# Attention by half chunks in two turns between the output products of a hybrid decoder layer

## The chip, the cores and the metric

The kernel runs on one core of one Trainium2 chip. Its engines are TensorE (PE in the profile, its weight loads PEld), VectorE (DVE), ScalarE (ACT), GpSimd (POOL) and SyncE (SP), which issues most DMAs. The metric is the device time of one execution in microseconds (us), as the median of the runs shown.

## The reference, cut to what matters

One layer: a normalised input is projected once, three head groups work on the result, and one output projection follows. Two of the groups are attentions:

```
q, k, v      8 query heads, 2 key/value heads (4 queries each), head_dim 64, 4096 tokens
window:      banded blocks of 128 queries against 256 keys (the block before and its own),
             mask 0 <= i + 128 - j < 128, softmax with one sink logit per head, * silu(gate)
memory:      4 heads of 64 against 256 memory tokens, softmax, * silu(gate)
y = concat(conv 256, window 512, memory 256) @ w_out;   out = x + rmsnorm(y) * norm_post
```

A second, small batch (8 x 8 tokens against cached keys) goes through the same layer, and the new keys, values and states are returned.

## The kernel before, in words

**Stages.** Three phases compute the input projection (line L368, tiles `c`), the last of them together with the memory keys and the attention of the first 256 tokens. Up to about 930 us that is all; the rest is attention and output projection, and this is the part that changes.

**Precision.** Most products are made from a high and a low part of each operand in the float32r type. For the window scores a head's 128 contraction rows hold the query's high part in one half of 64 rows and its low part in the other, against the key's high part (part 0 of `kst`) in both halves, and then against the key's low part (part 1): two products of 128 rows x 256 keys for each head and block of 128 queries. The products with the values (`wo`) are plain float32.

**Chunks and halves.** The 4096 tokens are 16 chunks of 256 (`Chunk`, c from 0), each with two blocks of 128 queries (i = 0, 1). I call block i of chunk c the half h = 2c + i. Halves 0 and 1 are done in the input projection, so that 30 are left.

**Steps of one half.**
- Window scores `ws` (L1246): for each key/value head (kvh) 4 heads x 2 parts, 16 products into four one-bank PSUM tiles. ACT copies the own block's columns (L1248), DVE puts the previous block's columns over them under a mask (L1249), then maximum (L1251), exponentials (L1259, sink L1256), sum, reciprocal and factor (L1264), all in tile `sm`.
- Transposes `wt` (L1269) of `sm`; ACT copies them out (L1271), and two selections on POOL make the two triangles (L1276, L1279).
- Memory scores `xs` (L1182) for 2 heads, maximum (L1183), exponentials (L1186), factor on POOL (L1191), transposes `xt` (L1197), and copies out, half by DVE and half by ACT (L1201).
- Products with the values (`wo`, L1088 for memory, L1218 and L1224 for the window) in column tiles and 64 x 64 tiles of TensorE, two or four at once, and two gates on DVE (L1170, L1227).

**Order.** `pairs` cuts a chunk into eight units (window and memory in turn, one for each kvh or memory head). `Pipe.start` begins one unit, puts the transposes of the unit begun two starts earlier on the queue, and after each pair its products. The output projection of a block of 128 tokens, `Block.run`, is 2 parts of 24 products of 512 columns (`y`, L1492); it calls `start` ahead of k = 2 and k = 6 of each part (0, 2, 4, 6 in the first two blocks), so at four places in a block. A scheduler at build time fixes the order of the instructions on every engine of this stage.

**Memory.** PSUM's eight banks: tags `s`, `t` and `z` (the `y` sums) with two banks each, and `pv`, one tile of two banks. Keys and queries of chunk c + 1 are loaded from DRAM by POOL's queue while chunk c is worked on, the gates (`mix`) by SP's. The small batch's attention (`sample_mem`, `sample_window`) is spread over blocks 26 to 30.

Of the kernel before, what the change touches and what calls it, by code (L numbers as in the profile page):

```python
# [52 lines left out]
def hybrid_layer(ctx: ExitStack, tc: tile.TileContext, a: dict):  # L53
# [951 lines left out]
    def open_attention():  # L1005
# [7 lines left out]
        ps = {tag: ctx.enter_context(tc.tile_pool(name=f"ps{tag}", bufs=1 if tag == "pv" else 2, space=bass.MemoryType.PSUM))  # L1013
              for tag in ("s", "t", "z", "pv")}
# [19 lines left out]
    def psum(tag, name):  # L1034
        if ps is None:
            return third["ps"].tile([P, 512], F32, tag="m", name=name)
        if tag == "pv":

            return ps[tag].tile([P, 2, 512], F32, tag=tag, name=name)[:, 0]
        return ps[tag].tile([P, 512], F32, tag=tag, name=name)  # L1040
# [6 lines left out]

    class Pipe:

        def __init__(self):
            self.waiting, self.due, self.t = [], {}, 0

        def add(self, pair):

            left, right, both = pair
            self.waiting += [(left, None), (right, both)]

        def start(self):
            values, transposes, factors = self.due.pop(self.t, ([], [], []))
            at = lambda n: self.due.setdefault(self.t + n, ([], [], []))
            if self.waiting:
                unit, both = self.waiting.pop(0)
                next(unit)
                at(1)[2].append(unit)
                at(2)[1].append(unit)
                if both is not None:
                    at(3)[0].append(both)  # L1070
            for fn in values:
                fn()
            for unit in (*transposes, *factors):
                next(unit, None)
            self.t += 1

        def drain(self):
            while self.waiting or self.due:
                self.start()
# [10 lines left out]
    class Chunk:  # L1090


        def __init__(self, c):
            self.c = c
            self.t0 = NS + CT * c
            self.ts = slice(self.t0, self.t0 + CT)
# [18 lines left out]
        def load_queries(self):  # L1115

            self.q = self.pool("q").tile([P, 12, CT], F32R, tag="q", name=f"q{self.c}")
            for part in range(2):
                for hh in range(2):
                    half = hh if part == 0 else 1 - hh  # L1120
                    G.dma_start(self.q[half * 64 : half * 64 + 64, hh::2, :],  # L1121
                                  qd[part, 1:7, hh * 64 : hh * 64 + 64, self.ts].rearrange("j p n -> p j n"))
# [34 lines left out]
        def cross_pair(self, j, band_values):  # L1157
# [4 lines left out]
            def both():  # L1162
                banks = ps["pv"].tile([P, 2, 512], F32, tag="pv", name=f"wo{c}_{j}") if c else None
# [10 lines left out]
        def cross_unit(self, h, pts):  # L1174
            c, nb = self.c, CT // P
            q = self.q[:, h]
            p = work([P, nb, 256], "p", f"xp{c}_{h}")
            mx, nm, den, rd = (tiny.tile([P, 4], F32, tag=n, name=f"x{n}{c}_{h}") for n in ("mx", "nm", "den", "rd"))
            s = psum("s", f"xs{c}_{h}").rearrange("p (b k) -> p b k", b=nb)
            for i in range(nb):  # L1180
                for part in range(2):
                    TE.matmul(s[:, i, :], q[:, i * P : i * P + P], third["mk"][:, part, h, :], start=part == 0, stop=part == 1)  # L1182
# [4 lines left out]
            V.reciprocal(rd[:, :nb], den[:, :nb])  # L1187
            yield 1
            for i in range(nb):

                G.tensor_scalar(p[:, i, :], p[:, i, :], rd[:, i : i + 1], 0.5, op0=ALU.mult, op1=ALU.mult)  # L1191
            yield 1
            pt = work([P, 2, CT], "xpt", f"xpt{c}_{h}")
            for kt in range(2):
                t = psum("t", f"xt{c}_{h}_{kt}")
# [253 lines left out]
    class Block:  # L1449
# [26 lines left out]
        def run(self, last, start, split, starts):  # L1476
# [6 lines left out]
            for p, (c0, c1) in enumerate(parts):  # L1483
                if p == 1:
                    split()
# [197 lines left out]
```

## Time and profile before

| what | value |
|---|---|
| median of 3 runs | 1538.47 us (1533.01 to 1540.08) |
| the profiled execution: its own time, span of the core | 1536.4 us, 1534.7 us |
| granted TensorE clock | 1.00 |
| busy: PE, PEld, DVE, ACT, POOL | 99%, 91%, 75%, 52%, 25% |
| DMA | 306.28 MB, mean 200 GB/s |

The profiled execution is one run; its own time is 2.1 us under the median. Busy time of PE is taken from modelled ends of pipelined matmuls, so that a matmul's duration (0.28 us for 256 columns) is longer than the distance from its start to the next one's. The text below reads distances between starts.

### The profile page before, as it was taken

The numbers are of one execution on the slowest core, as the hardware profiler recorded it, in microseconds if no ns is written. First come the engines' busy times: TensorE is split into PE (matmuls) and PEld (weight loads), VectorE is DVE, ScalarE is ACT, GpSimd is POOL, SyncE is SP. The second block draws the span as 40 slices with busy tenths as digits, with TensorE's granted clock in tenths as the row PEclk, the third lists the DMA queues.
The fourth block names the chain that finished last, engine by engine and source line by source line (L and its number), as shares of the span: only waits on it lengthen the run. The fifth ranks groups of instructions, "written<-read, shape, count | busy, mean of one in ns | idle before, by whom it ended". The sixth has DMA issues, their size and how long they took to land.

```text
span 1534.7 us, 30168 instructions
## 1 busy us (share of the span) xinstructions
PE 1521.5 (99%) x11341; PEld 1399.5 (91%) x11341; DVE 1145.5 (75%) x2055; ACT 805.7 (52%) x2039; POOL 376.1 (25%) x603
## 2 busy tenths in 40 slices
PE   9999999999999999999999999999999999999998
PEld 9999999999999999999999998788888888888877
DVE  6788887899988777897777678766666666666743
ACT  6675665475322222354454447655666556565632
POOL 0223332211300000000101203544444444444310
PEclk9999999999999999999999999999999999999999
DMA  9989999878855333677877789977777777777333
GB/s 265 194 222 225 283 284 266 272 242 298 193 181 180 126 126 126 220 230 280 227 273 230 229 293 254 231 161 153 156 148 148 151 162 149 158 160 150 130 110 96
DMA packets 177942, 306.28 MB, mean 200 GB/s; under 512 B 33925, under 2 KB 107653, under 8 KB 177765
## 3 DMA queue, kind: packets, MB, share of 16 engines
q1 hardware_dynamic: 130901, 227.38, 48.2%
q0 software_dynamic: 46176, 75.92, 25.5%
q8 instruction: 90, 1.47, 0.4%
q10 hardware_dynamic: 720, 1.05, 0.2%
q14 instruction: 55, 0.45, 0.1%
HBM read 197.23 MB, written 108.05 MB: 199 GB/s over the span
## 4 chain that ended last, share of the span: by engine, by line
PE 86%; DMA 7%; DVE 4%; issue 1%; ACT 1%; POOL 1%; SPq 0%; ACTq 0%; DVEq 0%; POOLq 0%
PE c L368 47%; PE y L1492 23%; PE ws L1246 4%; DMA nat<-in_x_p 3%; DMA md<-th 2%; PE wo L1088 2%; PE wt L1269 2%; PE xs L1182 2%; PE xt L1197 2%; PE wo L1218 2%; PE wo L1224 1%; PE mem_acc L789 1%; DMA qd<-z 1%; DVE z L375 1%; DMA xr<-in_x_p 0%
## 5 line engine op out<-in xcount | busy, mean ns | idle before, releaser
L1492 PE MATMUL y<-wo,mh 128*128 128x512 f32 (+1 forms) x1040 | 349.8, 399 | 0.0
L375 DVE TENSOR_TENSOR z<-c,z 128x520 f32<-128x520 f32 (+1 forms) x308 | 194.5, 646 | 79.2 <-PE c L368 78.2
L1492 PEld LDWEIGHTS y<-wo,mh 128*128 128x128 f32 x1040 | 194.3, 188 | 39.2 <-issue 2.4
L1492 PE MATMUL y<-wo,ml 128*128 128x512 f32 (+1 forms) x520 | 201.6, 388 | 0.0
L1259 ACT ACTIVATE sm<-sm,wnm 128x128 f32<-128x128 f32 x256 | 99.5, 390 | 61.0 <-DVE wnm L1253 60.2
L1191 POOL TENSOR_SCALAR xp<-xp,xrd 128x256 f32<-128x256 f32 x128 | 74.4, 588 | 209.6 <-DVE xrd L1187 209.6
L1492 PEld LDWEIGHTS y<-wo,ml 128*128 128x128 f32 x520 | 98.2, 189 | 16.3
L1183 DVE TENSOR_REDUCE xmx<-xs 128x2 f32<-128x512 f32 x64 | 44.1, 689 | 59.2 <-PE xs L1182 59.1
L1271 ACT COPY wpt<-wt 128x512 f32<-128x512 f32 x64 | 37.3, 582 | 88.1 <-PE wt L1269 85.6
L1246 PEld LDWEIGHTS ws<-kst,q 128*128 128x128 f32 x512 | 69.9, 190 | 5.3 <-ACT xp L1186 0.7
L1499 DVE TENSOR_TENSOR yn<-y,gpost 128x512 f32<-128x512 f32 (+1 forms) x66 | 45.1, 683 | 39.6 <-PE y L1492 39.3
L1246 PE MATMUL ws<-kst,q 128*128 128x256 f32 x512 | 73.0, 283 | 0.4 <-ACT xp L1186 0.4
L1500 ACT ACTIVATE y<-y 128x512 f32<-128x512 f32 (+1 forms) x66 | 38.6, 584 | 64.2 <-DVE yn L1499 64.2
L737 POOL CAST wmask<-negs 128x256 uint8<-128x256 f32 x1 | 0.9, 864 | 268.3 <-ACT z L377 268.3
L1279 POOL TENSOR_SCALAR_AFFINE_SELECT wpt<-wpt 128x512 f32<-128x512 f32 x64 | 52.7, 824 | 42.1 <-ACT wpt L1271 39.1
L1186 ACT ACTIVATE xp<-xs,xnm 128x256 f32<-128x256 f32 x128 | 58.8, 464 | 7.1 <-DVE xnm L1184 7.1
L1121 POOL DMA_DIRECT2D q<-qd x64 | 42.8, 674 | 70.6 <-DVE wo L186 60.9
L276 ACT ACTIVATE nat<-nat 104x1024 f32<-104x1024 f32 x40 | 42.3, 1057 | 26.1 <-DMA nat<-in_x_p 26.1
L1510 DVE SCALAR_TENSOR_TENSOR xr<-yn,yst,xr 128x1024 f32<-128x1024 f32 (+2 forms) x34 | 43.4, 1280 | 15.5 <-POOL yst L1506 13.2
L1110 POOL DMA_DIRECT2D kst<-qd x64 | 38.6, 616 | 63.5 <-PE xt L1197 41.4
L1249 DVE COPY_PREDICATED sm<-wmask,ws 128x256 f32<-128x256 uint8 x124 | 52.2, 437 | 2.5 <-ACT sm L1248 2.1
L1276 POOL TENSOR_SCALAR_AFFINE_SELECT wpv<-wpt 128x512 f32<-128x512 f32 x62 | 40.2, 648 | 50.6 <-ACT wpt L1271 50.5
(961 smaller groups left out, 5095.5 us busy)
## 6 DMA issues: line engine op xcount, KB each, us to landing
q<-qd POOLq DMA_DIRECT2D x64, 384.0 KB, 7.9
xr<-in_x_p SPq DMA_DIRECT2D x32, 512.0 KB
nat<-in_x_p SPq DMA_DIRECT2D x39, 416.0 KB
o_yp<-xr SPq DMA_DIRECT2D x31, 512.0 KB
md<-th POOLq DMA_DIRECT2D x48, 260.0 KB, 7.9
qd<-zh SPq DMA_DIRECT2D x48, 260.0 KB
qd<-z SPq DMA_DIRECT2D x48, 260.0 KB
kst<-qd POOLq DMA_DIRECT2D x60, 192.0 KB, 5.6
```

The source lines that it names most:

```text
L368: TE.matmul(bank[:, :HW], l, r, start=first and i == 0, stop=last and i == 3 * KH - 1)
L375: add = lambda dst, other: V.tensor_tensor(dst, c, other, op=ALU.add)
L1183: V.tensor_reduce(mx[:, :nb], s, axis=AX.X, op=ALU.max)
L1186: S.activation(p[:, i, :], s[:, i, :], AF.Exp, bias=nm[:, i : i + 1], scale=SCALE, accum_out=den[:, i : i + 1])
L1191: G.tensor_scalar(p[:, i, :], p[:, i, :], rd[:, i : i + 1], 0.5, op0=ALU.mult, op1=ALU.mult)
L1246: TE.matmul(s3[:, hh, :], self.q[:, 4 + 2 * (2 * half + hh) + kvh, i * P : i * P + P], self.kst[:, 2 * kvh + part, i * P : i * P + 2 * P], ...
L1249: V.copy_predicated(sm[:, 2 * half : 2 * half + 2, :], third["wmask"], third["negs"] if first else s3[:, :, 0:P])
L1259: S.activation(sm[:, hh, :], sm[:, hh, :], AF.Exp, bias=nm[:, hh : hh + 1], scale=SCALE, accum_out=den[:, hh : hh + 1])
L1279: G.affine_select(p3, p3, pattern=[[0, 4], [1, P]], compare_op=ALU.is_ge, fill=0.0, base=0, channel_multiplier=-1)
L1492: TE.matmul(acc, self.hl[l][:, k], wo[k][c0 // 512][:, r, c0 % 512 : c0 % 512 + c1 - c0], start=j == 0, stop=j == passes * KT - 1)
L1499: V.tensor_tensor(yn[:m, c0:c1], acc[:m], gpost[:m, c0:c1], op=ALU.mult)
L1510: V.scalar_tensor_tensor(self.xr[:m, cs], yn[:m, cs], st[:m, 3:4], self.xr[:m, cs], op0=ALU.mult, op1=ALU.add)
```

## The change

- `Pipe`, `pairs` and the eight units of a chunk are gone for chunks after the first. Each half is now done in two turns. `first_half(h)`: window scores of half h, memory transposes of half h - 1, then the window softmax of h. `second_half(h)`: memory scores of h, products of h - 1, the transposes of the new values (every other half), window transposes of h, gates of h - 1.
- `Block.run` calls one turn ahead of k = 4 of each part: block b does the turns of half b + 4. In blocks 0 to 2 the table `EARLY` puts them closer.
- TensorE's instructions of blocks 0 to 25 stay in program order (`manual_schedule`); the other engines are still ordered by the scheduler.
- The low-key products of the window scores have 64 contraction rows instead of 128: only the half that holds the query's high part is multiplied by the key's low part (the low by low part is dropped). Heads of the first PSUM bank use rows 0 to 63, those of the second rows 64 to 127, in turn. For that the queries lie in another order of halves, and are loaded by six DMAs of 256 KB in place of four of 384 KB.
- PSUM: two tiles of two banks (`w`) shared by window scores, window transposes and products, one of two banks (`x`) for memory scores and transposes, two of one bank (`z`).
- Copies out of PSUM are made two banks at a time.
- In blocks 26 to 30 the small batch's stages are called at k = 1 and 3 of each part in place of 2 and 6.

```diff
-        ps = {tag: ctx.enter_context(tc.tile_pool(name=f"ps{tag}", bufs=1 if tag == "pv" else 2, space=bass.MemoryType.PSUM))
-              for tag in ("s", "t", "z", "pv")}
+        ps = {tag: ctx.enter_context(tc.tile_pool(name=f"ps{tag}", bufs=n, space=bass.MemoryType.PSUM))
+              for tag, n in (("w", 2), ("x", 1), ("z", 2))}
...
-                for hh in range(2):
-                    half = hh if part == 0 else 1 - hh
-                    G.dma_start(self.q[half * 64 : half * 64 + 64, hh::2, :],
-                                  qd[part, 1:7, hh * 64 : hh * 64 + 64, self.ts].rearrange("j p n -> p j n"))
+                for n, (i, j) in enumerate(((0, 1), (4, 3), (8, 5))):
+                    half = (n == 2) ^ part
+                    G.dma_start(self.q[64 * half : 64 * half + 64, i : i + 4, :].rearrange("p (j v) n -> p j v n", v=2),
+                                heads(part, j, self.ts))
...
+        def window_scores(self, i):
+            b = 2 * self.c + i
+            w = [two_banks("w", f"ws{b}_{kvh}") for kvh in range(2)]
+            tasks = [(kvh, j % 2, j // 2) for kvh in range(2) for j in range(4)]
+            out = lambda kvh, col, bank: w[kvh][:, bank, 256 * col : 256 * col + 256]
+            q = lambda kvh, col, bank: self.q[:, 4 + 2 * (2 * bank + col) + kvh, i * P : i * P + P]
+            k = lambda kvh, part: self.kst[:, 2 * kvh + part, i * P : i * P + 2 * P]
+            for kvh, col, bank in sorted(tasks):
+                TE.matmul(out(kvh, col, bank), q(kvh, col, bank), k(kvh, 0), start=col == 0, stop=True, skip_group_check=col > 0)
+            for kvh, col, bank in sorted(tasks):
+                r = slice(64 * bank, 64 * bank + 64)
+                TE.matmul(out(kvh, col, bank), q(kvh, col, bank)[r], k(kvh, 1)[r], start=False, stop=True,
+                          skip_group_check=True, tile_position=(64 * bank, 0))
+            self.ws = w
...
+    def first_half(h):
+        c, i = divmod(h, 2)
+        if c < NCH:
+            chunks[c].window_scores(i)
+        if 2 < h <= 2 * NCH:
+            chunks[(h - 1) // 2].memory_transposes((h - 1) % 2)
+        if c < NCH:
+            chunks[c].window_probabilities(i)
+            if i == 0:
+                chunks[c].values(chunks[c - 1].vts[2])
+                chunk_load(c + 1)
+            elif c + 1 < NCH:
+                chunks[c + 1].load_mix()
+    def second_half(h):
+        c, i = divmod(h, 2)
+        if c < NCH:
+            chunks[c].memory_scores(i)
+        banks = None
+        if 2 < h <= 2 * NCH:
+            banks = chunks[(h - 1) // 2].products((h - 1) % 2)
...
+        if c < NCH:
+            chunks[c].window_turns(i)
+        if 2 < h <= 2 * NCH:
+            chunks[(h - 1) // 2].gates((h - 1) % 2, banks)
...
+    EARLY = {4: (first_half, 2), 12: (second_half, 2), 14: (first_half, 3), 20: (second_half, 3), 22: (first_half, 4),
+             28: (second_half, 4), 30: (first_half, 5), 36: (second_half, 5), 38: (first_half, 6)}
+    def starts_of(b):
+        steps = {n - 16 * b: (f_, h) for n, (f_, h) in EARLY.items() if n // 16 == b}
+        if b >= 2:
+            steps |= {4: (first_half, b + 4), 12: (second_half, b + 4)} if b > 2 else {12: (second_half, b + 4)}
+        return {(n // 8, n % 8): lambda f_=f_, h=h: f_(h) for n, (f_, h) in steps.items()}
...
+    turn = ExitStack()
+    turn.enter_context(tc.manual_schedule(engines={mybir.EngineType.PE}))
     for i in range(31):
-        run(i, late_start if i >= 26 else start, (0, 2, 4, 6) if i < 2 else (2, 6))
+        if i == 26:
+            turn.close()
+        starts = starts_of(i)
+        run(i, starts | ({(p, k): late for p in range(2) for k in (1, 3)} if i >= 26 else {}))
```

More of the change, by code (lines that the diff above doesn't have):

```diff
@@ L1046, in work @@
         return places[tag].tile(shape, F32, tag=tag, name=name)
[L1048 to L1079, printed above, removed]
     def both_values(o, left, right):
@@ L1474, in split, with run @@
             self.hl = [hi, lo]
-        def run(self, last, start, split, starts):
+        def run(self, last, starts):
             b, m = self.b, self.m
@@ L1550, in run @@
             blocks[i].split()
[L1551 removed]
+        if i == 1:
+            starts[1, 4] = lambda before=starts[1, 4]: (before(), split())
+        blocks[i].run(i == len(blocks) - 1, starts)
     stages = [sample_mem(0), sample_mem(1), sample_window()]
```

181 lines of the change are left out of this document (123 added, 58 removed).

## The prediction

> **What bounds the kernel now.** I read the page first, for the bound.
>
> ```profile
> span 1534.7 us, 30168 instructions
> PE 1521.5 (99%) x11341; PEld 1399.5 (91%) x11341; DVE 1145.5 (75%) x2055; ACT 805.7 (52%) x2039; POOL 376.1 (25%) x603
> PE 86%; DMA 7%; DVE 4%; issue 1%; ACT 1%; POOL 1%; SPq 0%; ACTq 0%; DVEq 0%; POOLq 0%
> PE c L368 47%; PE y L1492 23%; PE ws L1246 4%; DMA nat<-in_x_p 3%; DMA md<-th 2%; PE wo L1088 2%; PE wt L1269 2%; PE xs L1182 2%; PE xt L1197 2%; PE wo L1218 2%; PE wo L1224 1%; PE mem_acc L789 1%; DMA qd<-z 1%; DVE z L375 1%; DMA xr<-in_x_p 0%
> ```
>
> The chain of waits is TensorE itself, 86%, with `c` and `y` as its largest parts; the window scores, which the change makes cheaper, are 4%. So the question is how many microseconds of TensorE's own sequence go, and whether a wait comes in. The next views are the windows (all instructions, then line L1492 alone; the columns are the window, its length, busy time and count of each engine, clock, DMA) and one row of the chain in order of time.
>
> ```profile
> 930.27:1001.99 71.72, 69.29 (x438) 54.69 (x437) 56.13 (x148) 47.25 (x185) 37.56 (x63) 1.00 1.12 250
> 1199.37:1236.06 36.69, 36.69 (x228) 30.01 (x227) 24.72 (x63) 21.73 (x81) 16.75 (x26) 1.00 0.79 156
> 930.27:1001.99 71.72, 37.67 (x144) 25.79 (x145) 1.00 1.12 250
> 1199.37 2.77 PE y L1492 x12
> ```
>
> The second row is two blocks in the steady stretch: PE is busy for all of it at clock 1.00, DVE for 67%, ACT 59%, POOL 46%. A block is 36.69 / 2 = 18.35 us. Twelve `y` products take 2.77, one 0.230, so 48 of them 11.06, and 7.29 is the attention of a half. The first row is blocks 0 to 2 from the end of the input projection (144 `y`): DMA is over full share there, and PE has 2.4 us idle.
>
> **What the four starts cost.** The timeline of PE in a steady block shows every kind of transition (start, length to the last end, instructions merged).
>
> ```profile
> 1154.81 1.11 PE L1246 MATMUL ws<-kst,q 128*128 128x256 f32 x8
> 1155.76 0.60 PE L1197 MATMUL xt<-ident,xp 128*128 128x128 f32 x4
> 1156.12 0.48 PE L1492 MATMUL y<-wo,mh 128*128 128x512 f32 x1
> 1156.44 0.39 PE L1492 MATMUL y<-wo,ml 128*128 128x512 f32 x1
> ...
> 1158.71 0.39 PE L1492 MATMUL y<-wo,mh 128*128 128x512 f32 x1
> 1158.94 0.63 PE L1182 MATMUL xs<-mk,q 128*128 128x256 f32 x4
> 1159.50 1.08 PE L1088 MATMUL wo<-xpt,mkv 128*64 128x256 f32 x8
> 1160.42 0.60 PE L1218 MATMUL wo<-wpv,vt 128*64 128x256 f32 x4
> 1160.85 0.60 PE L1218 MATMUL wo<-wpt,vt 128*64 128x256 f32 x4
> 1161.38 0.43 PE L1224 MATMUL wo<-wpv,vt 64*64 64x256 f32 x2
> 1161.39 0.43 PE L1224 MATMUL wo<-wpt,vt 64*64 64x256 f32 x2
> 1161.65 0.38 PE L1224 MATMUL wo<-wpv,vt 64*64 64x256 f32 x2
> 1161.66 0.38 PE L1224 MATMUL wo<-wpt,vt 64*64 64x256 f32 x2
> 1161.97 0.66 PE L1269 MATMUL wt<-ident,sm 128*128 128x128 f32 x4
> ```
>
> Going into a start costs nothing: `y` to `xs` is 0.23, the pitch of `y`. Coming out, the last transpose is followed by `y` at once (1156.12 against 1155.76 plus three pitches of 0.11) and that first `y` takes 0.32, together 0.35 where 0.11 + 0.23 = 0.34 is normal. So halving the number of starts, the change's most visible part, I cost at nothing.
>
> **The low-key pairs.** Eight `ws` in 1.11, the last 0.28 long: a pitch of 0.83 / 7 = 0.119, 0.95 for eight. Half of a half's sixteen become 64-row tiles, in neighbours that use different rows and PSUM banks. No 64 x 128 float32r tile is in this trace. The nearest rows are the two L1224 pairs, 64 x 64 tiles with different rows and banks: four start within 0.02 us and the set of four takes one pitch. I take full overlap: four pairs at 0.119, 0.48, a saving of 0.47 per half. The bounds are 0.47 and nothing (pairs one after the other).
>
> Against that stand two changes of tiling mode. From 128*64 to 64*64, the last L1218 pair starts at 1160.85 + 0.60 - 0.38 = 1161.07, the next would follow at 1161.285 (pitch (1160.85 - 1160.42) / 2 = 0.215), and it starts at 1161.38; its first set takes 0.27 in place of 0.215. Together 0.15. Back to 128*128 the same way: 0.10 + 0.06 = 0.16. Into 128*64 from `xs`: 0.09 + 0.05 = 0.14. So the new 64-row set costs 0.14 + 0.16 = 0.30. The Trainium skill, in TensorEngine Tiling (Array Packing), Key Properties, says that a change of tiling mode, not merely of tile, drains TensorE; it gives no price, and this trace agrees, with 0.14 to 0.16 each time. By its speedup of up to 2x alone the pairs would bring 0.47; with the drain a third of that is left. Net 0.47 - 0.30 = 0.17 per half, 30 halves: **-5.1 us**.
>
> **New waits in TensorE's program order.** What waits now holds back every `y` behind it. The stage's pieces:
>
> ```profile
> L1259 ACT ACTIVATE sm<-sm,wnm 128x128 f32<-128x128 f32 x240 | 93.3, 390 | 58.2 <-DVE wnm L1253 57.3 <-DVE xnm L1184 0.7
> L1191 POOL TENSOR_SCALAR xp<-xp,xrd 128x256 f32<-128x256 f32 x124 | 72.5, 592 | 194.0 <-DVE xrd L1187 194.0
> L1249 DVE COPY_PREDICATED sm<-wmask,ws 128x256 f32<-128x256 uint8 x120 | 50.7, 437 | 2.5 <-ACT sm L1248 2.1
> L1279 POOL TENSOR_SCALAR_AFFINE_SELECT wpt<-wpt 128x512 f32<-128x512 f32 x61 | 50.0, 820 | 2.9
> L1264 DVE TENSOR_TENSOR sm<-sm,wrd 128x512 f32<-128x512 f32 x60 | 41.4, 690 | 1.0
> L1251 DVE TENSOR_REDUCE wmx<-sm 128x4 f32<-128x512 f32 x60 | 40.7, 678 | 0.1
> L1121 POOL DMA_DIRECT2D q<-qd x60 | 40.2, 673 | 69.7 <-DVE wo L186 60.9 <-PE wt L1269 6.1 <-PE y L1492 1.6
> L1276 POOL TENSOR_SCALAR_AFFINE_SELECT wpv<-wpt 128x512 f32<-128x512 f32 x61 | 39.1, 641 | 45.9 <-ACT wpt L1271 45.9
> L1271 ACT COPY wpt<-wt 128x512 f32<-128x512 f32 x60 | 35.0, 583 | 88.1 <-PE wt L1269 85.6 <-POOL sq L1324 2.4
> L1201 DVE COPY xpt<-xt 128x256 f32<-128x256 f32 x62 | 26.0, 419 | 9.4 <-PE xt L1197 9.3
> ...
> 1155.44 0.40 ACT L1259 ACTIVATE sm<-sm,wnm 128x128 f32<-128x128 f32 x1 [2.63 <-DVE wnm L1253]
> 1157.09 0.35 ACT L1248 COPY sm<-ws 128x256 f32<-128x256 f32 x1
> ```
>
> The last two rows enclose four exponentials and the sink's: 1.65. In the steady stretch the second tile's softmax, counted from the first `ws`: scores of the first tile at 1.5, its copy 0.58, two masks of at most 0.87 (twice 437 ns), the `xpt` copy 0.84, two maxima 1.36, small operations 0.2, exponentials 2 x 1.65, sum, reciprocal and factor 1.0: 10.6 us. TensorE arrives there after 1.73 (scores with both mode changes), 0.87 (`xt`), 24 `y` 5.53, `xs` 0.94, products 2.6, four `wt` 0.5: 12.1. So no wait, with 1.5 to spare. The memory path has more: maxima, four exponentials and four factors of 0.59, some 6.5 with the queues, against 11.6 to its transposes. The shared tiles `w` come free in time too: copies of `wt` (2 x 0.58) and gates have the 12 `y` after the turn and 12 of the next block, 5.5 us.
>
> The two more query loads per chunk cost POOL 2 x 0.67 in 36.7 us, 46% busy; bytes are the same. Fewer, wider copies take 0.3 from ACT and about 0.35 from DVE per half, off TensorE's path.
>
> **The start.** Here turns stand 6 and 18 `y` apart. Before, this stretch holds 144 `y`, the scores and `wt` of five halves and the rest of four: 33.2 + 4 x 7.29 + 3.8 = 66.1 of steady cost, so 71.72 has 5.6 us of loss, in idle time and in mode changes of an order in which the scheduler mixed `wo` with `xs`. After, the first softmax meets DVE's leftovers, which stand ahead of it in the built order too:
>
> ```profile
> 932.44 3.75 DVE L409 TENSOR_TENSOR z<-z,zh 128x520 fp32r<-128x520 f32 x6
> 936.11 1.23 DVE L1473 TENSOR_TENSOR ml<-place,mh 128x1024 fp32r<-128x1024 f32 x1
> 937.24 0.78 DVE L1249 COPY_PREDICATED sm<-wmask,ws 128x256 f32<-128x256 uint8 x2
> ```
>
> From 937.3, masks and maxima end near 940, exponentials at 943.3, the second factor at 944.4; TensorE wants its two tiles from 941.6 on: 2.3 us of stall. Then the second memory factor stands on POOL behind four selections (2 x 0.64 + 2 x 0.82): 1.5 us at the transposes of half 2. The four later close turns I give 1.7 us together, since with 18 `y` TensorE arrives at 10.7, as the softmax ends. Sum 5.5 against 5.6: -0.1, uncertain by 4 either way.
>
> **Sum.** -5.1 - 0.1, and the tail's sample stages, moved by one or two k, at nothing: -5.2. On the profiled run's own 1536.4 (its span and 1.7 around it) that is 1531.2; that run stands 2.1 under the median of 1538.47, on which I forecast 1533. That is -0.34%, within the 0.5% (7.7 us) that a measurement of this kernel tells from no change.
>
> **Rivals.** One more row first, of the weight loads of the 64 x 64 tiles.
>
> ```profile
> 1161.38 0.14 PEld L1224 LDWEIGHTS wo<-wpv,vt 64*64 64x64 f32 x2 [0.38 <-issue]
> ```
>
> - The start gains: in program order the mode changes of the mixed order go, and most waits are shorter than I made them. For it: the idle time there is only 2.4 of 5.6. Price: down to 1 us of stall, so -5.1 - 4.6 = -9.7, 1529. Chance 0.20.
> - The pairs do not pair: weight loads of 128 columns, two in a pair, go one after the other. The 64 x 64 rows speak against it (two loads in 0.14); that no float32r row tile is in the trace speaks for it. Then +0.30 per half, +9.0: 1547; half overlapped at a 0.215 pitch, +0.21 and +6.3: 1545. Chance 0.12. The Trainium skill, in TensorE: Matmul & The Clock Gate, LDWEIGHTS, says that a load takes its columns' time whatever its rows, 107 ns for 128 by its formula, an estimate of 0.21 for a pair if loads share one path; the trace has two of the 64-column loads in 0.14 together, which a shared path does not explain.
> - Slower: the window softmax becomes TensorE's wait at `wt` in every block. It decides above 12.1 us after the first `ws`; each microsecond beyond stalls some 25 blocks that have both turns. For it: ACT and DVE also serve `y`, `mh`, `ml` and `xr` between its steps. One us late is +25, so 1558. Chance 0.12.
> - The start loses twice my stalls: +5.5, 1538.5. Chance 0.08.
>
> **How the numbers follow.** The forecast has 0.48. Faster by over 0.5%: the first rival 0.20 and 0.10 of the forecast's own spread, 0.30. Slower: the softmax wait 0.12 and 0.07 of the pairs, 0.19. The rest, 0.51, is within. The range goes from the first rival less the 4 us by which the start is uncertain to pairs that do not overlap: 1525 to 1548; it leaves out the softmax wait.
>
> **What would show it.** Right: in the steady stretch a block of 18.18 us in place of 18.35; the 64-row scores in the timeline as x2 within 0.01 us; no idle time of PE before `wt` or `xt` after block 3; blocks 0 to 2 in 67 to 75 us. Wrong: low-key products 0.12 apart; `wt` waiting on DVE `sm` in every block; a start over 80 us.

## The result, and the profile after

The changed kernel takes 1557.70 us, the median of six runs (1553.53 to 1562.16), against 1535.26 for the kernel before in six runs; the ratio is 1.0141, with a 95% interval of 1.0126 to 1.0156. The forecast was 1533 (1525 to 1548): it is slower by 22 us where a change of -5 was forecast, and outside the range. The profiled execution is the slowest of the six, 1562.16 us with a span of 1560.3.

The page of the changed kernel, span and busy times:

```profile
span 1560.3 us, 30035 instructions
PE 1525.2 (98%) x11341; PEld 1391.5 (89%) x11341; DVE 1145.7 (73%) x1965; ACT 792.5 (51%) x1949; POOL 394.6 (25%) x635
```

PE's busy time has grown by less than 4 us while the span grew by 25.6, so most of the loss is idle time of TensorE. The windows say where (window, its length, busy time and count of PE, PEld, DVE, ACT and POOL, clock, DMA; each stretch is cut at the start of the last `y` product ahead of its block, some 0.23 us early everywhere). First the kernel before: blocks 3 to 25, and block 26 up to the start of the last one. Then the changed kernel: from the end of the input projection to the start of block 3, and the same two stretches.

```profile
1001.99:1424.34 422.35, 422.35 (x2602) 345.28 (x2601) 284.95 (x713) 250.30 (x923) 192.37 (x300) 1.00 0.75 153
1424.34:1520.48 96.14, 96.14 (x574) 74.98 (x573) 53.50 (x129) 40.46 (x132) 19.27 (x44) 1.00 0.37 120
```

```profile
937.82:1012.40 74.58, 69.01 (x441) 53.93 (x440) 56.58 (x135) 47.27 (x176) 39.60 (x69) 0.98 1.13 250
1012.40:1444.66 432.26, 421.43 (x2599) 335.20 (x2598) 283.66 (x641) 236.80 (x846) 200.97 (x321) 1.00 0.72 151
1444.66:1545.16 100.50, 97.78 (x574) 75.09 (x573) 54.97 (x125) 40.34 (x126) 23.38 (x47) 0.98 0.32 103
```

The changed kernel's first row answers to the 71.72 in the prediction's fence. So the start is +2.9, the steady stretch +9.9 (PE idle for 432.26 - 421.43 = 10.8, before not at all), the tail from block 26 +4.4, and the last block +0.9. The clock of 0.98 in the start and in the tail is one spell of 3.41 us at half the clock in each, which costs 1.7 us (last section). The remaining 7.6 of the 25.6 stand ahead of the attention: the input projection ends at 937.8 instead of 930.3. Its code is the same; I come back to it.

In the steady stretch, PE's timeline, and its waits from 1095 to 1425 us (us in total, times, the longest):

```profile
1182.33 1.11 PE L1292 MATMUL ws<-kst,q 128*128 128x256 f32 x8
1183.37 0.74 PE L1295 MATMUL ws<-kst,q 64*128 64x256 f32 x8
1184.04 1.09 PE L1326 MATMUL xt<-ident,xp 128*128 128x128 f32 x8
...
1194.24 0.60 PE L1338 MATMUL wt<-ident,sm 128*128 128x128 f32 x4
1195.51 0.63 PE L1338 MATMUL wt<-ident,sm 128*128 128x128 f32 x4 [0.67 <-DVE sm L1260]
```

```profile
PE wt L1338 <- DVE sm L1260: 9.9, 18, 0.7
```

The eight 64-row products take 0.74 us, less than the eight full ones: they run in pairs, as forecast. In the trace the two of a pair start 0.003 to 0.004 us apart; the first pair takes 0.22, the next ones 0.12 each. But the second tile of `wt` waits for the factor on `sm`, in each of the 18 blocks. That is the third rival of the prediction. Measured from the first `ws` of a half, the second factor on DVE ends, block by block (worked out from the starts and ends in the trace; TensorE, when nothing holds it, wants the tile at 12.1 in blocks with an odd number and at 12.35 in even ones):

| kernel | b3 | b4 | b5 | b6 | b7 | b8 | b9 | b10 |
|---|---|---|---|---|---|---|---|---|
| changed, `sm` ready at | 9.94 | 10.85 | 11.22 | 12.32 | 12.56 | 13.02 | 12.57 | 13.05 |
| changed, length of the block | 18.04 | 18.28 | 18.03 | 18.42 | 18.65 | 19.11 | 18.65 | 19.14 |

This table is the key. Blocks 3 to 5 have the period that was forecast, and in block 3 the softmax is ready 2.2 us early. But it comes later from block to block, until the time to spare is used up in block 6; from then on the block lasts 18.65 and 19.13 in turn. Something off TensorE has a period of 18.89 of its own, 0.74 above TensorE's 18.15 (417.39 us for 23 blocks in run 1, where TensorE waits for nothing). One turn of it in the timelines of DVE and POOL, and then DVE's wait for `xr` from 1095 to 1425 us:

```profile
1181.26 0.17 DVE L1153 RECIPROCAL xrd<-xden 128x2 f32<-128x2 f32 x1 [0.83 <-ACT xp L1152]
...
1182.68 1.45 DVE L1545 TENSOR_TENSOR ml<-place,mh 128x1024 fp32r<-128x1024 f32 x1 [0.67 <-ACT mh L1544]
1184.06 0.20 DVE L1574 TENSOR_SCALAR yst<-yst 128x1 f32<-128x1 f32 x1
1186.45 1.28 DVE L1579 SCALAR_TENSOR_TENSOR xr<-yn,yst,xr 128x1024 f32<-128x1024 f32 x1 [2.19 <-POOL yst L1575]
1187.65 1.34 DVE L1306 COPY_PREDICATED sm<-wmask,ws 128x512 f32<-128x512 uint8 x2
...
1194.67 0.69 DVE L1260 TENSOR_TENSOR sm<-sm,wrd 128x512 f32<-128x512 f32 x1
1195.28 0.68 DVE L1149 TENSOR_REDUCE xmx<-xs 128x2 f32<-128x512 f32 x1
```

```profile
1181.53 0.93 POOL L1161 TENSOR_SCALAR xp<-xp,xrd 128x256 f32<-128x256 f32 x2 [0.87 <-DVE xrd L1153]
1182.42 0.63 POOL L1278 TENSOR_SCALAR_AFFINE_SELECT wpt<-wpt 128x512 f32<-128x512 f32 x1
1183.01 1.61 POOL L1275 TENSOR_SCALAR_AFFINE_SELECT wpv<-wpt 128x512 f32<-128x512 f32 x1
1184.58 0.65 POOL L1092 DMA_DIRECT2D q<-qd  x1
1185.23 0.65 POOL L1278 TENSOR_SCALAR_AFFINE_SELECT wpt<-wpt 128x512 f32<-128x512 f32 x1
1185.84 0.57 POOL L1575 TENSOR_TENSOR yst<-yst,mhalf 128x1 f32<-128x1 f32 x1
```

```profile
DVE xr L1579 <- POOL yst L1575: 31.9, 17, 2.2
```

Read it as a round. DVE's `xrd` lets POOL do its factors `xp`; behind them, in POOL's order, stand selections, a query load and the power `yst`; DVE's residual `xr` waits for that power (2.19 us idle), and the masks of the next half stand behind `xr`, although the last scores were issued at 1183.8; maxima, exponentials and factors follow, and the next `xmx` comes right behind the last factor, at 1195.28. From there to `xrd` and POOL again. TensorE is in none of these steps. The last line gives the wait of `xr` over 17 blocks.

One step of the round is longer than it need be: the selection at 1183.01 takes 1.61 us, the next one 0.65. It began while DVE computed `ml`. In each of the 23 blocks from 3 to 25 one selection is slow like this, in the kernel before in 11 of the 23. By the trace some 0.96 us of a turn of the round is this delay (1.61 - 0.65), more than the 0.74 by which it is too long. No run changes it by itself, so whether the round would be short enough without it is not shown.

### The profile page after: what moved, and what is told of

It reads as the page before. It is cut to its first block, busy times and chain, and to the rows that moved or that the text cites. A ratio compares the mean times of both kernels' runs of the same rounds, so it can differ in the third digit from the quotient of the medians.

```text
span 1560.3 us, 30035 instructions
## 1 busy us (share of the span) xinstructions
PE 1525.2 (98%) x11341; PEld 1391.5 (89%) x11341; DVE 1145.7 (73%) x1965; ACT 792.5 (51%) x1949; POOL 394.6 (25%) x635
## 5 line engine op out<-in xcount | busy, mean ns | idle before, releaser
L1561 PE MATMUL y<-wo,mh 128*128 128x512 f32 (+1 forms) x1040 | 338.9, 396 | 0.0
L1161 POOL TENSOR_SCALAR xp<-xp,xrd 128x256 f32<-128x256 f32 x128 | 60.2, 480 | 251.9 <-DVE xrd L1153 250.1
L1092 POOL DMA_DIRECT2D q<-qd x96 | 60.3, 637 | 108.3 <-DVE wo L186 60.4
L1330 ACT COPY xpt<-xt 128x512 f32<-128x512 f32 x30 | 17.6, 587 | 109.1 <-DVE xpt L1330 109.1
L1275 POOL TENSOR_SCALAR_AFFINE_SELECT wpv<-wpt 128x512 f32<-128x512 f32 x62 | 51.0, 837 | 6.3 <-ACT wpt L1270 6.3
L1153 DVE RECIPROCAL xrd<-xden 128x2 f32<-128x2 f32 x64 | 10.6, 166 | 56.6 <-ACT xp L1152 56.6
L377 ACT COPY z<-c 128x520 f32<-128x520 f32 (+1 forms) x44 | 24.3, 553 | 51.6 <-PE c L368 48.5
L1338 PE MATMUL wt<-ident,sm 128*128 128x128 f32 x240 | 36.6, 281 | 14.2 <-DVE sm L1260 11.7
L407 ACT CAST zh<-z 128x520 fp32r<-128x520 f32 x56 | 33.4, 625 | 33.2 <-DVE z L375 29.5
L1338 PEld LDWEIGHTS wt<-ident,sm 128*128 128x128 f32 x240 | 26.2, 142 | 24.9 <-ACT y L1569 14.6
```

The costliest lines, as they stand in the source:

```text
L1092: G.dma_start(self.q[64 * half : 64 * half + 64, i : i + 4, :].rearrange("p (j v) n -> p j v n", v=2), heads(part, j, self.ts))
L1161: G.tensor_scalar(p[:, i, :], p[:, i, :], self.rds[h][:, i : i + 1], 0.5, op0=ALU.mult, op1=ALU.mult)
L1275: G.affine_select(pv.rearrange("p (h q) -> p h q", h=4), p3, pattern=[[0, 4], [-1, P]], compare_op=ALU.is_gt, fill=0.0, base=0, channel_mu ...
L1338: TE.transpose(tw[:, kvh, hh * P : (hh + 1) * P], self.sms[kvh][:, hh, :], ident)
L1561: TE.matmul(acc, self.hl[l][:, k], wo[k][c0 // 512][:, r, c0 % 512 : c0 % 512 + c1 - c0], start=j == 0, stop=j == passes * KT - 1)
```

## The experiments

Ratios are to the kernel before on the same chip. Where the start (blocks 0 to 2) is given, it counts from the end of the input projection, 71.7 us in the kernel before; the expectations of runs 5, 7 and 10 count it from the first `y`, 70.9 there. In the other kernels the two are the same within 0.1 us, except in runs 4 and 5.

**1. Take `xr` out of the round.**

```diff
+            def finish(after=None):          # yst, the power, xr and its store
+                    with tc.issue_after(after): V.scalar_tensor_tensor(self.xr ...
...
+        # run(i): called in the next block, behind first_half
+            starts[LATE] = lambda: (first(), late_end(chunks[(i + 4) // 2].sink_sum))
```

> The changed kernel with one edit: in blocks 3 to 25 the end of an output block (sum of squares, POOL's power, the residual `xr` on DVE) is issued behind the sink sums `wes` of the next window softmax instead of ahead of its masks. Theory: in blocks 7 to 25 the period is set by a round through the queues of DVE, ACT and POOL (memory maxima, exponentials, factors on POOL, two selections of each window tile, POOL's power, `xr`, masks, maxima, exponentials, factor), 18.65 and 19.13 us in turn, and TensorE (18.18 of its own work) waits for it at the second tile of `wt`. The edit takes 2.19 (DVE waiting for POOL's power) and 1.28 (`xr`) out of it: masks then start with the copies of `ws`, about 2.2 to 2.8 us after the first `ws` instead of 4.9 and 5.3, the factor ends 2.4 us earlier, no idle time before `wt`, blocks at 18.18. Blocks 3 to 25 418 us instead of 432, total 1557.7 - 14 = 1544. Rival 1, TensorE's own order or the 64-row products cost the time: the masks move, the blocks stay at 18.9, total 1557. Rival 2, the late `xr` holds its tile and so the loads and stores, a new wait: blocks at 18.4 to 18.7, total 1548 to 1554.

Measured: 1536.51, ratio 0.9999 (0.9986 to 1.0012). Blocks last 18.04 and 18.28 in turn from block 3 to block 25. DVE's longest wait from 1095 to 1408 us, and two rows of its timeline:

```profile
DVE sm L1306 <- ACT sm L1305: 38.2, 17, 2.5
```

```profile
1175.18 1.35 DVE L1306 COPY_PREDICATED sm<-wmask,ws 128x512 f32<-128x512 uint8 x2 [2.15 <-ACT sm L1305]
...
1178.63 1.28 DVE L1582 SCALAR_TENSOR_TENSOR xr<-yn,yst,xr 128x1024 f32<-128x1024 f32 x1
```

DVE now waits for the scores, not the scores for DVE; `sm` is ready at 9.94 in every block from 3 to 25 but one (10.13), and PE waits for nothing there. The theory holds: blocks 3 to 25 take 417.39 (-14.9, expected -14), and both rivals are out. The tail takes 96.75 (-3.8). What else the two profiles differ by is not the edit's: the input projection ends 4.3 earlier here, and the start takes 73.30 (-1.3). Run 12, in the changed kernel's order, has a start of 73.4 too; both lack the half-clock spell.

**2. Take the query loads off POOL's queue**, and leave `xr` where it is.

```diff
-                    G.dma_start(self.q[...], heads(...))
+                    (DMA if self.c > 2 else G).dma_start(f(self.q[...]), f(heads(...)))
```

> The changed kernel with the six query loads of each chunk from 3 on put on SP's queue (as raw 32-bit words) instead of POOL's. Theory (the round through DVE, ACT and POOL sets the period): in every second block one query load of 0.65 us lies between the selections ahead of POOL's power, so the 19.13 us blocks fall to about 18.5 and the 18.65 us blocks stay: ten times 0.65, total about 1551. If both query loads of such a block count, 1545. Rival, POOL's queue is not in the round (its idle times absorb them): no change, 1557. Other rival, the loads come earlier on SP and collide with its stores and loads: slower, over 1560.

Measured: 1538.69, ratio 1.0018 (1.0004 to 1.0032). The gain is larger than expected: blocks of 18.04 and 18.28 again, up to block 24. The built orders of TensorE and ACT are those of the changed kernel, DVE's differs in one instruction of the start, and POOL's in the loads and what they had pushed aside. DVE's wait for the power is still there, shorter (1095 to 1405 us):

```profile
DVE xr L1579 <- POOL yst L1575: 20.6, 17, 1.5
```

`sm` is ready at 9.94 in block 4 and at 11.49 in block 24, 0.08 later from block to block: the round is 18.23, just above TensorE's 18.15, and the time to spare lasts for nearly the whole stretch. So the six loads, and the order of selections that goes with them, lengthened the round by 0.66 per block, 1.3 in two blocks; and a round 0.74 too long instead of 0.08 costs 14.5 us in blocks 3 to 25 (432.3 against 417.8).

**3. TensorE ordered by the scheduler.**

```diff
-    turn.enter_context(tc.manual_schedule(engines={mybir.EngineType.PE}))
```

> The changed kernel without the order by hand: TensorE's instructions of blocks 0 to 25 are ordered by the scheduler, as in the kernel before; turns, tiles, pairs and all else as changed. Theory (the round of DVE, ACT and POOL is too long): TensorE's own order matters little, DVE still has `xr` ahead of the masks, so blocks stay near 18.9 and the total near 1557, within 5. Rival, the program order is what costs (a scheduled order puts `y` products where `wt` would wait): blocks at 18.2 to 18.4, total 1535 to 1543.

Measured: 1557.50, ratio 1.0139 (1.0120 to 1.0157). Blocks of 18.67 and 19.13 from block 11 on, as changed, and 431.6 us for blocks 3 to 25 against 432.3. So TensorE's order is not the cause in the steady stretch. That the totals agree so well is partly luck: the start takes 81.2 us here against 74.6 (one idle time of 5.9), while the input projection ends at 928.6 in this profile and not at 937.8.

**4. The pairs alone, in the kernel before.**

```diff
+                for hh in range(2):
+                    for half in range(2):
+                        r = slice(64 * half, 64 * half + 64)
+                        TE.matmul(ss[half][:, 256 * hh : 256 * hh + 256], q(half, hh)[r], k(1)[r], start=False, stop=True,
+                                  skip_group_check=True, tile_position=(64 * half, 0))
```

> The kernel before with one part of the change alone: low-key products as 64-row tiles in pairs, with the six query loads that they need. There the two key/value heads are separate units, so a half has two sets of two pairs and four mode changes. By the forecast's own terms: four pairs save 0.47 per half, two sets cost 2 x 0.30 = 0.60, so +0.13 per half, +4 in 30 halves: 1535.3 + 4 = 1539. Rival 1, a mode change costs nothing where the queue is full: -0.47 x 30 = -14, 1521. Rival 2, the two more query loads on POOL cost as in the changed kernel, 0.65 in every second half on top: 1549.

Measured: 1555.99, ratio 1.0128 (1.0105 to 1.0151), far beyond every expectation. Blocks of 18.65 and 18.84, +0.39 to the kernel before, and 82.9 us for the start against 71.7. The two sets of a block in PE's timeline:

```profile
1185.89 0.63 PE L1249 MATMUL ws<-kst,q 128*128 128x256 f32 x4
1186.45 0.50 PE L1253 MATMUL ws<-kst,q 64*128 64x256 f32 x4
1186.89 0.66 PE L1199 MATMUL xt<-ident,xp 128*128 128x128 f32 x4
...
1190.20 0.95 PE L1249 MATMUL ws<-kst,q 128*128 128x256 f32 x4
1191.08 0.50 PE L1253 MATMUL ws<-kst,q 64*128 64x256 f32 x4
```

Four full products take 0.56 up to the pairs in the first set, 0.88 in the second: there the product into the second bank starts 0.33 behind the first, as soon as DVE's masked copy out of that bank ends. The order that pairs need takes both banks from the beginning. But this wait stands only in every second block (0.84 to 0.89 there, 0.56 in all other sets of blocks 3 to 25), so it is 0.16 of the +0.39 in the mean. The other 0.23 is what two sets cost by run 6's price: 2 x 0.35 for the mode changes less the 0.47 saved. One set for a half instead of two is thus what makes pairs affordable. The 11 us that the start lost show waits of 3.0 at `xs`, 1.5 and 1.7 at `xt`, and two spells of 3.41 us at half the clock; I did not separate them further than by the next run.

**5. The six loads alone, in the kernel before** (the part of the change that loads queries).

```diff
-                    G.dma_start(self.q[half * 64 : half * 64 + 64, hh::2, :], ...                 # 4 of 384 KB
+                    G.dma_start(self.q[64 * half : 64 * half + 64, i : i + 4, :].rearrange(...), ...   # 6 of 256 KB
```

> The kernel before with the six query loads of 256 KB per chunk in place of four of 384 KB, and nothing else. It tells what of the 20 us that the pairs cost in the kernel before belongs to the loads. Theory: the loads are hidden in the steady stretch (blocks stay at 18.36; the 0.39 us per block that the pairs added are 0.1 of mode changes and some 0.3 of waiting for the second of two score banks), and cost at most 2 us in the start, where POOL and DMA are busy: total 1536 to 1538. Rival: the two more issues on POOL's queue delay its factors and selections in every second block, and in the start: blocks of 18.36 and 18.8 in turn, blocks 0 to 2 at 80 us instead of 71, total 1545 to 1550.

Measured: 1541.16, ratio 1.0028 (1.0013 to 1.0043). Blocks stay at 18.27 and 18.45, the start takes 73.3 (+1.6). So in the steady stretch of the old order POOL's queue has room for them, and most of run 4's 11 us in the start is not the loads'. The total is above the 1536 to 1538 of the theory and below the rival's. This profile (1536.18) is the fastest of ten executions, 5.0 under their median, so where the rest of the 4.6 us over the kernel before lies isn't shown.

**6. The price of the pairs, with the late `xr`.**

```diff
-                TE.matmul(out(kvh, col, bank), q(kvh, col, bank)[r], k(kvh, 1)[r], ... tile_position=(64 * bank, 0))
+                TE.matmul(out(kvh, col, bank), q(kvh, col, bank), k(kvh, 1), start=False, stop=True, skip_group_check=True)
```

> The kernel with the late `xr`, with low-key products of 128 rows again (the low by low part is added, as before). It prices the pairs where TensorE alone sets the period: 18.15 us with pairs. By the forecast's terms (0.47 saved, 0.30 for two mode changes) the block is 18.32, 30 halves give +5.1, total 1541.5. Rival 1, mode changes are cheaper than that: up to 18.62 and +14, 1550. Rival 2, the pairs bring nothing, and the gain in the steady stretch comes from the order of the turns: 18.15, total 1536.5.

Measured: 1537.18, ratio 1.0013 (1.0003 to 1.0023). Blocks of 18.16 and 18.39, 18.27 in the mean against 18.15: the pairs bring 0.12 a half, 3.7 in thirty. The forecast had 0.17; if 0.47 is saved as forecast, the two mode changes cost 0.35 and not 0.30. The medians of runs 1 and 6 differ by less than that, since each moves by some us from run to run outside this stretch.

**7. The first turns spread evenly.**

```diff
-    EARLY = {4: (first_half, 2), 12: (second_half, 2), 14: (first_half, 3), 20: (second_half, 3), 22: (first_half, 4), ...
+    EARLY = {2: (first_half, 2), 8: (second_half, 2), 12: (first_half, 3), 18: (second_half, 3), 22: (first_half, 4),
+             28: (second_half, 4), 32: (first_half, 5), 38: (second_half, 5), 42: (first_half, 6), 48: (second_half, 6)}
```

> The kernel with the late `xr`, and the first turns spread evenly: a half every 10 steps of three products of the output projection (18 `y` to the closing turn, 12 to the next) up to half 7, instead of 8 steps (18 and 6) up to half 6. The first half opens two steps earlier. With the late `xr` alone the start loses 2.4 us to the kernel before (73.3 for blocks 0 to 2 against 70.9), with waits of TensorE of 1.7 and 0.6 at the first two `wt`, 1.1 at `ws`, 1.0 at `xt`. Theory: the waits at `ws` and `xt` come from turns that stand 6 `y` apart and go with 12; the first `wt` waits for leftovers of the input projection on DVE and stays: 2 us less up to the start of block 4 (89.4 from the start of block 0 instead of 91.35), total 1534.5. Rival: the engines are behind by what is left over from the input projection, and the waits only move: 91, total 1536.5.

This kernel and the next leave something out: block 4 enters the output projection before the values of memory heads 2 and 3 have been multiplied in. The instructions are the same, but one dependence is missing, so the start is not quite that of the full computation. Measured: 1541.09, ratio 1.0035 (1.0022 to 1.0049). 99.97 us up to block 4, not 89.4. TensorE waits 3.4 and 1.0 at the first `wt`: opened two steps earlier and closed after 18 `y` instead of 24, the first half still finds DVE at the leftovers. The theory falls, the rival is right and too mild.

**8. All of it with the loads on SP.** (Runs 1, 2 and 7 together, the late `xr` up to block 26.)

```diff
-        if 3 <= i < 25:
+        if 3 <= i < 27:
```

> All that helps together: the late `xr` (in blocks 3 to 26), the first turns spread evenly, the query loads on SP's queue. Theory: the late `xr` and the loads on SP shorten the same round, which with either is already shorter than TensorE's 18.15, so they do not add in the steady stretch; in the tail (blocks 26 to 28) and the start POOL's freed time may give 1 us. Total 1533 to 1535, 0.1 to 0.2% under the kernel before. Rival: the loads on SP cost 2 us as in the run with them alone (1538.7 against 1536.5): 1536 to 1537.

Measured: 1539.92, ratio 1.0029 (1.0016 to 1.0042); the start of run 7 costs more than the rest gains.

**9. Four query loads on POOL.**

```diff
-                for n, (i, j) in enumerate(((0, 1), (4, 3), (8, 5))):
-                    half = (n == 2) ^ part
+                for i, j, n in ((0, 1, 4), (8, 5, 2)):
+                    half = (i == 8) ^ part
```

> The changed kernel with the queries of a chunk loaded by four DMAs on POOL's queue again (two of 512 KB, two of 256 KB) instead of six of 256 KB. With the loads off POOL's queue altogether (the run on SP's queue) the masks slipped by some 0.10 us per block against the window scores, 1.5 us in 15 blocks; in the changed kernel the slip is 0.74 (18.89 less 18.15). Theory: each issue on POOL's queue that stands between the factors, the selections and the power lengthens the round by its 0.65; two issues fewer per two blocks leave 0.74 - 0.65 = 0.1 of slip, the 1.7 us to spare last to about block 20, and only the last blocks wait: blocks 3 to 25 at 18.15 to 18.25, 418 to 420 us, total 1537 to 1540. Rival 1, only some issues lie in the round, and the merged ones do not: 18.6, total 1550. Rival 2, larger loads land later: `ws` waits for its queries, over 1557.

Measured: 1532.83, ratio 0.9980 (0.9967 to 0.9994): this one edit turns the change from 1.4% slower to 0.2% faster. Blocks 3 to 25 take 417.39, and `sm` is ready at 9.94 or 9.49 in turn from block 5 to block 25. No slip at all is better than the 0.1 expected, because the scheduler answered too: in every second half it put each tile's second selection right behind its first on POOL, and the first tile's maximum ahead of the second tile's mask on DVE. Slow selections beside `ml` are 11 here, not 23. So this run prices the two issues together with the order that follows; what two issues cost alone isn't shown. Run 2 is the cleaner price (of all six loads), this one the better kernel.

**10. The first `ml` behind the first softmax, with the late `xr`.**

```diff
+            starts[0, 4] = lambda before=starts[0, 4]: (before(), blocks[1].split(chunks[1].sink_sum))
```

> The kernel with the late `xr`, and in the start one step moved: the low part `ml` of block 1 (1.2 to 1.45 us on DVE, right ahead of the first masks) is issued behind the sink sums of the first window softmax. Theory: the first masks wait for DVE, not for the scores; they start 1.3 us earlier, the first two waits at `wt` (1.7 and 0.6) fall to about 1 together, and the slower clock of the 5 us after them goes: blocks 0 to 2 in 71 instead of 73.3, total 1534.5. Rival, DVE's leftovers of the input projection set the masks anyway: the same 73.3, 1536.5.

Measured: 1533.56, ratio 0.9992 (0.9977 to 1.0008). The masks of the first half start 3.1 instead of 4.2 after its `ws`, block 0 lasts 19.2 instead of 20.9, but block 2 26.8 instead of 25.1, and the start is 73.65, not 71: the gain moved into a later wait.

**11. What helped, together** (runs 1, 9 and 10, the late `xr` up to block 26, and the small batch's stages at k = 2 and 6).

```diff
-        run(i, starts | ({(p, k): late for p in range(2) for k in (1, 3)} if i >= 26 else {}))
+        run(i, starts | ({(p, k): late for p in range(2) for k in (2, 6)} if i >= 26 else {}))
```

> What should help, together: late `xr` in blocks 3 to 26, four query loads, the late `ml` of block 1, and the small batch's stages at k = 2 and 6 as in the kernel before. Theory: steady blocks at 18.15 (-5 to the kernel before), start as in the run with the late `ml` alone (0 to -2 by one query load less), block 28 back from 20.2 to about 19.2 (-1): total 1531.5 to 1533.5, 0.2 to 0.3% under the kernel before. Rival: the start and the tail keep their losses (+2.4, +0.6), and the total stays at 1536.

Measured: 1531.39, ratio 0.9973 (0.9960 to 0.9986), the lowest median of all, though its interval overlaps run 9's. Its windows, start, blocks 3 to 25 and tail:

```profile
931.28:1001.91 70.63, 67.17 (x441) 52.65 (x439) 54.42 (x135) 47.39 (x176) 36.45 (x63) 1.00 1.16 264
1001.91:1419.30 417.39, 417.39 (x2600) 335.66 (x2599) 283.58 (x644) 240.96 (x851) 184.93 (x301) 1.00 0.77 155
1419.30:1516.07 96.77, 96.42 (x575) 73.94 (x573) 52.75 (x121) 39.28 (x121) 18.65 (x44) 1.00 0.34 111
```

With four loads the start gets its gain (-1.1 to the kernel before), the steady stretch gives -5.0, and PE is busy for all of it. Moving the small batch's stages brought nothing (the tail is 96.77 against 96.75 in run 1, which has the late `xr` only up to block 24).

**12. The pairs undone in the changed kernel** (run 6's edit, without the late `xr`; the built order is the same on every engine).

> The changed kernel with low-key products of 128 rows again (the low by low part is added, as before), six query loads and `xr` ahead of the masks as changed. With the late `xr` this cost 0.12 us per half (18.27 instead of 18.15). Theory: here the round of DVE, ACT and POOL sets the period, whatever TensorE has to do below it: from block 8 on 18.65 and 19.13 in turn as with the pairs, the waits at `wt` 0.12 shorter; only blocks 3 to 6 and the stretches outside are longer, under 1 us together: total 1557 to 1559. Rival, the stalls add to TensorE's own work: 0.12 x 30 = 3.5 more, 1561.

Measured: 1551.73, ratio 1.0109 (1.0083 to 1.0134). In the steady stretch the theory is met to the hundredth: 18.65 and 19.13 again, though TensorE has 0.12 more to do in each half, and its waits from 1095 to 1415 us shrink by as much (line L1336 there):

```profile
PE wt L1336 <- DVE sm L1260: 7.5, 17, 0.6
```

TensorE does not set the period here. The total is 6 us under the expectation, and the profile puts it outside the stretch: the input projection ends at 929.6, not at 937.8, and there is no half-clock spell in the start or the tail.

## Why the prediction was wrong, point by point

- **Number of starts, at nothing:** nothing speaks against it. With the round out of the way the block is 18.27 with full products against 18.36 before, so all of the change but the pairs gained 0.09 there.
- **Low-key pairs, -5.1:** the mechanism was right, and the size nearly: 0.12 per half (run 6) instead of 0.17, since two mode changes cost 0.35 (if the pairs save 0.47). The rival "pairs do not pair" is out.
- **"So no wait, with 1.5 to spare":** the chain itself was right. With DVE free it takes 9.94 (forecast 10.6), and TensorE wants the tile at 12.1 to 12.35 (forecast 12.1). What failed is the assumption under it, that the chain starts with the scores. I added up one pass, and never closed the loop, that is, never asked whether the queues of DVE, ACT and POOL, one pass behind the other, get round in less than TensorE's 18.15. They need 18.89, so from block 7 on the masks start 4.8 to 5.3 us after the first `ws` instead of 2.2. The rival had the right place and the right words ("ACT and DVE also serve `y`, `mh`, `ml` and `xr` between its steps"), but as a delay of fixed size; in truth it is a period, and decides at 18.15 us per half and not at 12.1 us after `ws`. From it 23 blocks x 0.74 - 2.2 to spare = 14.8; run 1 takes back 14.9 there. That the rival's price, 1558, meets the measured 1557.7 is luck: it puts one microsecond on each of 25 blocks, while of the measured loss some 15 us come from the round in blocks 3 to 25, set against 5 gained there, and the rest stands in the start, the tail and the input projection.
- **The two more query loads, priced at nothing** ("2 x 0.67 in 36.7 us, 46% busy"): queue loads were priced by POOL's busy share, and that is wrong. POOL had idle time, but not where the loads stood: POOL waited for DVE's `xrd`, and then had factors, selections, a load and the power to do one behind the other while DVE waited. Run 2 shows the price of all six, 14.5 us in blocks 3 to 25. With two fewer and the order that followed, run 9 gains 14.9 there. That two loads alone tip it isn't shown, and with none at all the round is still 18.23.
- **The start, -0.1:** the sum of the stalls was right (PE idle 74.58 - 69.01 = 5.6, forecast 5.5), in part by luck: 1.6 of it is at `ws`, which waited for the shared tiles `w` to come free (ACT's copies of `wt`, a gate on DVE), and there none was forecast. The 5.6 of loss that I set against it in the kernel before did not go: 2.4 of it was idle time, the rest is in PE's busy time, and that has hardly changed (69.29, 69.01, of which 1.7 is the half-clock spell). Hence +2.9, within the 67 to 75 given.
- **The tail, at nothing:** +4.4. 3.8 of it are gone in run 1; 1.7 of these are the half-clock spell, behind an idle time of 2.0 at 1492, and the rest goes with the round, which goes on there among the small batch's steps.
- **Left open:** the input projection, whose code is the same, ends at 937.8 in the profile of the changed kernel and at 927.7 to 933.5 in the thirteen other profiles, in whatever kernel. Against the kernel before, its trace loses 5.0 us up to the 801st `c` product (109.1 against 104.1), gains 1.7 back by the 5601st (682.0 against 678.7), and loses 4.3 behind it. In each of these two stretches with a loss TensorE has one long idle time, 2.2 us at 85 (waiting for DVE's `mix_s`) and 2.6 at 781 (for DVE's `mk`), with 3.41 us at half the clock behind it: 4.8 + 3.4 = 8.2 together. The kernel before has neither; five of the other profiles have one or both, of 1.1 to 2.5 us. So the 7.6 us are no work of the change, and belong in part to the profiled run, which is 4.5 above its own median. Why DVE is late there in some executions is not settled.

That run 9 meets the 1533 of the forecast is luck. The forecast counted from 1538.47, which six runs put at 1535.26; it had -5.2, and run 9 has -2.6: -5.0 in blocks 3 to 25, +1.4 in the start, +1.2 in the tail. What holds of it is the steady stretch, where the round is short enough: -5.0 where 23 x 0.17 = 3.9 was forecast.

## What to carry to other kernels

When TensorE is the bound, check every other engine for its period and not for its busy share: follow its queue from one pass to the same place in the next, through the engines that it waits for, and compare that length with TensorE's. A round that is 0.1 too long may be hidden for twenty passes by what there is to spare, and one that is 0.7 too long shows after four; so look at how a wait grows from pass to pass, not at one pass. An issue of a DMA on a busy engine's queue is an instruction like others (0.62 to 0.65 us of POOL for each query load in the changed kernel), and an instruction that waits (here `xr` for a power on POOL) should stand behind the work that does not depend on it.

## What was not expected of the hardware

TensorE's idle times in the changed kernel were often followed by a lower clock. PE alone, five windows of the changed kernel and two cut to the slow spells; then three of the kernel with the late `xr`, around the same instructions:

```profile
85.00:90.00 5.00, 2.91 (x16) 0.87 1.05 268
90.00:95.00 5.00, 5.00 (x36) 0.79 0.87 217
780.00:785.00 5.00, 2.40 (x21) 1.00 0.98 344
785.00:790.00 5.00, 5.00 (x32) 0.66 0.67 220
950.00:955.00 5.00, 3.39 (x13) 0.73 1.30 363
88.69:92.10 3.41, 3.41 (x18) 0.50 1.01 272
785.01:788.42 3.41, 3.41 (x18) 0.50 0.67 260
```

```profile
85.00:90.00 5.00, 3.69 (x28) 1.00 1.03 291
780.00:785.00 5.00, 3.90 (x33) 1.00 0.95 373
785.00:790.00 5.00, 5.00 (x44) 1.00 0.64 183
```

After 2.6 us without work from 781 the five microseconds from 785 hold 32 products at a clock of 0.66, where 44 fit: 3.41 us of them are at half the clock, so the stall costs another 1.7. The changed kernel's profile has four such spells ahead of its last block (from 88.69, 785.01, 952.26 and 1494.98), each 3.41 us at 0.50. In the second kernel the waits at the first two places are 1.7 us each (partly ahead of these windows), and the clock stays at 1.00. The Trainium skill, in TensorE: Matmul & The Clock Gate, The HAM clock gate, names an idle window of some 3.4 us, free-running, ahead of half the clock. With free-running the trace agrees: the four spells start 204, 49 and 159 times 3.413 us apart. But 2.2 to 2.6 us without work were enough, and 1.7 with 0.5 to 0.6 behind it, early in the start, was followed by half the clock in three profiles (changed, runs 6 and 9) and not in three others (runs 1, 2 and 12).

Also not expected: a selection on POOL takes 1.61 us beside `ml` on DVE, and 0.65 alone (1183.01 and 1185.23 above). All 23 slow ones of blocks 3 to 25 began after `ml` had begun and ended 0.49 to 0.50 us behind its end, wherever in it they had begun; those that began ahead of `ml` took the usual 0.63.
